# Thirty-six seven-product quads instead of thirty-two in a hybrid attention and SSD layer

## The chip, the cores and the metric

The kernel runs on one core of a Trainium2 chip. The metric is device time in microseconds, the median of several executions. Matrix products run on TensorE (PE in the profile), elementwise work on VectorE (DVE), ScalarE (ACT) and GpSimd (POOL), and SyncE (SP) issues nearly all DMAs.

## What is computed

One layer on a sequence of 256 rows of width 2048, in float32:

```python
hn = rms_norm(x, norm_w)
proj = hn @ w_in                      # 2048 x 18496
q, k, v, z_a, z_s, xbc, dt_raw, g_a, g_s = split(proj)
o_a = dilated_attention(q, k, v) * silu(z_a)
xbc = silu(causal_conv(xbc));  xs, bm, cm = split(xbc)
y = ssd_scan(xs * dt, dt * a, bm, cm) + d_skip * xs
y = rms_norm(y * silu(z_s), ssm_norm_w)
merged = sigmoid(g_a) * (o_a @ w_attn_branch) + sigmoid(g_s) * (y @ w_ssm_branch)
out = rms_norm(x + merged @ w_out, final_norm_w)
```

The change touches three of the products: y @ w_ssm_branch, with 4096 rows of weights, and v and g_a, two 2048x2048 blocks of `proj`; o_a @ w_attn_branch and merged @ w_out run in the same way.

## The kernel before, in words

**Weights.** All weights lie in one array of units of 128x1024 (512 KB), in the order in which they are used, and are streamed through five buffers (`w<n>`, tag `w`, `W_BUFS`). float32 accuracy comes from three reduced products: ACT writes a rounded copy H of a unit (`h<n>`, L264), DVE the rest L = w - H (`l<n>`, L265), and `triple` (L459 to L461) multiplies xh by H, xh by L and xl by H, where xh and xl are the same two parts of the left operand. h and l have four buffers each.

**Quads.** The five products go through `gemm_pair`. It works on a pair of 512-wide blocks of columns at once (a pass; c is 0 for the first and 2 for the second), and in steps of two 128-row tiles of weights, a quad, whose units are numbered `first + 2 * q` and one more. A pass of ssm has 16 quads, one of v, ga (the gate g_a), attn or out has 8. A plain quad is the eight products of two by two blocks, 24 matmuls of 128x512. A quad in the table `S_QUADS` is done with seven products, 21 matmuls, on sums of the blocks (a Strassen scheme). Its left sums `sx_*` are made by `turn_x`, from two tiles of the left operand, and its right sums from the units `wa` and `wb`. On DVE such a quad is: wb minus wa (L514), la (L509), lc (L509), a second sum into wb (L520), a third into wa (L522), ltt (L509) and ltu (L509); ACT makes ha, hc, htt and htu. H and L of the sums, ht and lt, have two buffers each. Four of the seven products go to accumulators of their own (`pp_*`), which `fold` (L545 to L551) adds after the pass; the others and the plain quads go to `ps_*`. After a pass the four `ps_*` are added to the folded blocks: eight half-wide (128x512) additions on DVE in all.

**Sums made early.** For ga, attn and out, `sum_jobs` makes the first two right sums of each quad during the attention phase, one half-wide subtraction each, and stores them in DRAM (`t_ga0_2`, and so on); the quad then loads `wt` from there and needs neither L514 nor L520.

**Left sums made early.** `keep_left` makes sums in a temporary, `sxt_*`, as soon as their tiles of the left operand are there, and spills them to DRAM (`sxd_*`); `fetch_left` loads them back behind a named unit: POOL copies one column of that unit's H into the new tile, which makes the DMA wait until H is done. For y and x this is done in the scan phase, for the attention result o during attention. The temporary `sxt_o6` takes a buffer of `ht`.

**Order.** A scheduler with priorities arranges each engine's instructions; the conversions of the weights (L264, L265, L508 to L522) run under `tc.high_priority(L_AHEAD)`, ahead of their place in the text. The order of quads in a pass is `A_ORDERS` for attn, `V_ORDERS` for v, `G_ORDERS` for ga, `O_ORDERS` for out (None is 0 to 7). `behind_unit(n, f)` calls f when unit n is converted, with its H as the gate.

**The opening.** The first units w0 to w4 and the blocks of x are loaded one after another by SP (L595 to L599 for w0 to w3, `load_on` for w4). Unit n is followed by the load of unit n + 4.

The stages after the opening: the projections for the scan and its groups; ssm, v; sixteen heads of attention; ga, attn, out.

Of the kernel before, what the change touches and what calls it, by code (L numbers as in the profile page):

```python
# [10 lines left out]
F32R = mybir.dt.float32r  # L11
# [4 lines left out]
P = 128  # L16
# [20 lines left out]
DT_LAG, CB_LAG, TURN_LAG, GT_LAG, Y_LAG, S_LAG, M_LAG = 2, 5, 3, 2, 11, 2, 2  # L37
Y_AFTER = 0, 0
GS_BEFORE = {0: (0, 1), 4: (2,)}
A_ORDERS = {0: (0, 1, 2, 3, 4, 6, 5, 7), 2: (0, 2, 1, 4, 3, 6, 5, 7)}  # L40
V_ORDERS = {0: None, 2: None}
G_ORDERS = {0: None, 2: None}
O_LEFT = {0: {0: (0, 3), 4: (1, 5)}, 2: {}}
O_ORDERS = {0: (0, 1, 2, 4, 3, 6, 5, 7), 2: None}
RX_UNITS = {c: 16 + c for c in range(1, 8)}
NEG = -1.0e30
S_QUADS = {
    ("ssm", 0): (5, 7, 9, 11, 13), ("ssm", 2): (5, 7, 9, 11, 13),
    ("v", 0): (2, 4, 6), ("v", 2): (2, 4, 6), ("ga", 0): (2, 4, 6), ("ga", 2): (2, 4, 6),
    ("attn", 0): (2, 4, 6), ("attn", 2): (2, 4, 6), ("out", 0): (3, 5), ("out", 2): (3, 5),  # L50
}
SX_Y = S_QUADS[("ssm", 0)]
SX_X = (2, 4, 6)
O_BEHIND = 3, 5, 7, 7
SUMS_ATT = [(t, q) for t in [(n, c) for n in ("ga", "attn", "out") for c in (0, 2)] for q in S_QUADS[t]]
ATT_QUADS = S_QUADS[("attn", 0)]
LEFT_EVERY, ATT_EVERY = 11, 4
SUM_LAG = 3

# [52 lines left out]
FIRST = {}  # L112
# [72 lines left out]
def hybrid_block(ctx: ExitStack, tc: tile.TileContext, wall, xt, x, pk_d, cst_d, fw_d, out):  # L185
# [16 lines left out]
    XT = big.tile([P, KT, 2 * S], F32R, name="XT", tag="xm")  # L202
# [11 lines left out]
    loaded = {}  # L214
# [4 lines left out]
    def behind_unit(n, f):  # L219
        on_unit.setdefault(n, []).append(f)  # L220

    def ring(name):
        return stream.tile([P, UNIT], F32, name=name, tag="w", bufs=W_BUFS)

    def spill(kept, key, name, src, shape):
        kept[key] = dram.tile([P, *shape], F32, name=name, tag=name)
        nc.sync.dma_start(kept[key], src)
# [21 lines left out]
    def load(n, cuts=(0, UNIT)):  # L249
        if n not in loaded:  # L250
            loaded[n] = stream.tile([P, UNIT], F32, name=f"w{n}", tag="w", bufs=W_BUFS)
        for a, b in zip(cuts, cuts[1:]):
            nc.sync.dma_start(loaded[n][:, a:b], wall[n, :, a:b])
# [151 lines left out]
    def keep_left(key, x, spare, t):  # L405
# [2 lines left out]
        turn_x(sx, t.rearrange("p (n m) -> p n m", n=2), x, spare)  # L408
        spill(lefts, key, f"sxd_{key[0]}{key[1]}", sx.bitcast(F32), [2, 4 - spare, P])

    def new_sx(pool, bufs, spare, name):
        return pool.tile([P, 2, 4 - spare, P], F32R, name=f"sx_{name}", tag="sx", bufs=bufs)

    def fetch_left(kept, pool, bufs, key, x, spare, u):
        def get(behind):
            sx = new_sx(pool, bufs, spare, f"{key[0]}{key[1]}")
            gp.tensor_copy(sx[:, 0, 0, 0:1], behind)
            nc.sync.dma_start(sx.bitcast(F32), lefts[key])
            kept[key[1]] = left_parts(sx, x, spare)

        behind_unit(u, get)
# [161 lines left out]
    yT = [half_kts(f"yT{n}", f"yo0{n}") for n in "ab"]  # L583
# [18 lines left out]
    def fetch(dst, src, behind):  # L602
        gp.tensor_copy(dst[:, 0:1], behind)
        nc.sync.dma_start(dst, src)

    def load_on(u):
        load(u + 4)
        if u < 3:
            nc.sync.dma_start(xr[:, 2 * u + 10 : 2 * u + 12, :], xt[:, 2 * u + 10 : 2 * u + 12, :])
        if u == 3:  # L610
            nc.sync.dma_start(pk[:, KT:], pk_d[:, KT:])
# [31 lines left out]
    with tc.tile_pool(name="ssm", bufs=2) as sp:  # L643
# [206 lines left out]
        at = big.tile([P, UNIT], F32, name="at", tag="yo1b")  # L850
# [5 lines left out]

        for n, q in enumerate(SX_X):
            behind_unit(begin + 3 + n * LEFT_EVERY, lambda behind, q=q: left_x(q, behind))

        for g in range(GROUPS):  # L860
            if g:
                for c in GS_BEFORE.get(g, ()):
                    gates(("gs", c), th_s, XT)
                group = new_group(g)
                conv(collect(project(("B", g)), f"B{g}"), 32 + g, group[0], f"B{g}")
                conv(collect(project(("C", g)), f"C{g}"), 40 + g, group[1], f"C{g}")
                after(CB_LAG, lambda a=(g, *group): make_cb(*a), 1)
            cb = group[2]
            state = {"xs": [first["xs"]], "zs": [first["zs"]]} if g == 0 else {"xs": [], "zs": []}
            for t in range(max(4 * g, 1), 4 * g + 4):  # L870
                u, i = divmod(t, 2)
                acc = project(("xs", t))
                if i == 0:
                    state["xs"].append(new_pair(u, "xs"))
                if t % 4 == 3:
                    gate = 4 * len(GS_BEFORE.get(g + 1, ()))
                    after(TURN_LAG + gate * 3 // 4, lambda a=(g, state): turn(*a))

                    y_lag = Y_LAG + gate
                    for k in range(4):  # L880
                        after(GT_LAG + k if k < 3 else y_lag - 2, lambda a=(g, k, cb, state): decays(*a))
                    after(y_lag, lambda a=(g, state): scan(*a), 1)
                    for q in (2 * g, 2 * g + 1):
                        if q in SX_Y:
                            after(
                                y_lag + 2 + Y_AFTER[1] + q % 2 * 3,
                                lambda q=q, g=g: keep_left(
                                    ("y", q), two_kts(yT, q), 1, at if g < 6 else ring(f"sxt_y{q}")
                                ),
                            )  # L890
# [25 lines left out]
    xk = ctx.enter_context(tc.tile_pool(name="xk", bufs=1))  # L916
    sx_of_x = {}

    for n, q in enumerate(SX_X[:1]):
        fetch_left(sx_of_x, xk, 1, ("x", q), two_kts(XT, q), 0, FIRST[("ssm", 2)] + 24 + 4 * n)  # L920
    with tc.tile_pool(name="xp", bufs=1) as xp:
        sxs = {}

        for q in SX_Y:
            fetch_left(sxs, xp, len(SX_Y), ("y", q), two_kts(yT, q), 1, FIRST[("ssm", 0)] + 2 * (q - 3))
# [20 lines left out]
    xl = ctx.enter_context(tc.tile_pool(name="xl", bufs=1))  # L946
# [2 lines left out]
    behind_unit(FIRST[("v", 2)] + 1, lambda behind: fetch(dc, cst_d[:, :768], behind))  # L949
    if True:  # L950
        for n, q in enumerate(SX_X[1:]):
            fetch_left(sx_of_x, xl, 2, ("x", q), two_kts(XT, q), 0, FIRST[("v", 0)] + 1 + 2 * n)
        for c in (0, 2):
            es, prods = gemm_pair(("v", c), lambda kt: XT[:, kt, :], KT, sx_of_x, c == 2, order=V_ORDERS[c])
            dst = blocks(vt, c)
            fold(prods, dst)
            for d, e in zip(dst, es):
                ve.tensor_tensor(d, e, d, ALU.add)
    sx_of_o = {}

    with tc.tile_pool(name="att", bufs=2) as ap:
        ev = ap

        oaT = [half_kts("oaTa", "yo0a")]
# [52 lines left out]
        for h in range(NH):  # L1017
            q, k = (ap.tile([P, S], F32, name=f"{n}T{h}", tag=f"{n}T", bufs=2) for n in "qk")
# [12 lines left out]

        for n, q in enumerate(ATT_QUADS):
            fetch_left(
                sx_of_o, (xk, xl, xl)[n], (1, 2, 2)[n], ("o", q), two_kts(oaT, q), 0, FIRST[("ga", 2)] + 2 * O_BEHIND[n] + 1
            )
        for c in (0, 2):
            es, prods = gemm_pair(("ga", c), lambda kt: XT[:, kt, :], KT, sx_of_x, c == 2, order=G_ORDERS[c])
            open_gate(c, es, prods)
        tick(final=True)

    with tc.tile_pool(name="fin", bufs=2) as fp:
# [42 lines left out]
        spare = big.tile([P, 8, 512], F32, name="spare", tag="yo0a")  # L1084
        sxs = {}
# [4 lines left out]
        for c0 in (0, 2):  # L1090
# [67 lines left out]
```

## Time and profile before

| | us |
|---|---|
| Time before, median of 3 runs (lowest to highest) | 1392.53 (1391.42 to 1393.67) |
| The profiled execution, its own time | 1393.24 |
| Its span, from the first to the last instruction of the profile | 1391.4 |
| TensorE busy | 1379.0 (99%) |
| VectorE busy | 1120.5 (81%) |
| ScalarE busy | 819.3 (59%) |

How to read it: a row of the timeline has the start, the length, the engine, the line and the operation, and in brackets the idle time ahead of it with the instruction or DMA that ended it. A row of the groups has the count, the busy time and the mean in ns, then the idle time ahead of the group's instructions. A row of windows has each engine's busy time in that stretch. A matmul's length in these rows is modelled and overlaps the next one's; from start to start is what counts. `w<-in_wall` is the load of a weight unit, `sxd_o<-sxt_o` a spill of left sums, `wt<-t_attn` the load of a sum made early.

### The profile page before, as it was taken

How to read it: one execution, taken by the hardware profiler on the slowest of the kernel's cores; microseconds unless marked ns; L12 is line 12 of the kernel's file. 1: busy time of each engine (PE TensorE's matmuls, PEld its weight loads, DVE VectorE, ACT ScalarE, POOL GpSimd, SP SyncE). 2: the span in 40 equal slices, each digit the busy share in tenths (PEclk: the TensorE clock that was granted, in tenths of full speed). 3: DMA queues.
4: the chain of work that ended last, by engine and by line, in shares of the span. 5: the costliest groups of instructions: out<-in, count | busy, mean ns of one | idle time of the engine just before them, and what ended most of it. 6: DMA issues, size and time to landing. Idle time of an engine off the chain costs nothing.

```text
span 1391.4 us, 20301 instructions
## 1 busy us (share of the span) xinstructions
PE 1379.0 (99%) x7290; PEld 1173.6 (84%) x7290; DVE 1120.5 (81%) x1660; ACT 819.3 (59%) x1273; POOL 86.7 (6%) x154
## 2 busy tenths in 40 slices
PE   8999999999999999999999999999999999999997
PEld 7888888888888888888888888888888888888886
DVE  6897897787787887879688896777877678779897
ACT  7656676675667676765455454545545456556454
POOL 1300000000000000000000001111110000000121
PEclk9999999999999999999999999999999999999999
DMA  9766765756575666567566667888886556766764
GB/s 342 231 187 186 238 216 171 214 185 218 178 212 177 214 187 206 187 203 252 172 227 222 231 223 242 278 268 285 293 290 194 179 180 226 245 227 215 252 240 155
DMA packets 91685, 307.75 MB, mean 221 GB/s; under 512 B 10240, under 2 KB 12224, under 8 KB 91456
## 3 DMA queue, kind: packets, MB, share of 16 engines
q1 hardware_dynamic: 90864, 305.28, 67.5%
q8 instruction: 57, 0.93, 0.3%
q10 hardware_dynamic: 720, 1.18, 0.2%
q14 instruction: 44, 0.36, 0.1%
HBM read 290.75 MB, written 15.66 MB: 220 GB/s over the span
## 4 chain that ended last, share of the span: by engine, by line
PE 95%; DVE 2%; DMA 2%; ACT 1%; issue 0%; POOL 0%; SPq 0%; POOLq 0%; DVEq 0%; ACTq 0%
PE ps_zs L317 8%; PE ps_xs L317 8%; PE ps_zs L320 4%; PE ps_za L317 4%; PE ps_k L317 4%; PE ps_q L317 4%; PE ps_xs L320 4%; PE ps_ssm L459 3%; PE ps_ssm L460 3%; PE ps_ssm L461 3%; PE ps_q L320 2%; PE ps_k L320 2%; PE ps_za L320 2%; PE ps_gs L402 2%; PE ps_gs L400 2%; PE ps_gs L401 2%
## 5 line engine op out<-in xcount | busy, mean ns | idle before, releaser
L265 DVE TENSOR_TENSOR l<-w,h 128x1024 fp32r<-128x1024 f32 (+1 forms) x420 | 506.9, 1211 | 196.1 <-ACT h L264 194.4
L264 ACT ACTIVATE h<-w 128x1024 fp32r<-128x1024 f32 (+1 forms) x420 | 438.5, 1049 | 372.6 <-issue 94.3
L317 PE MATMUL ps_zs<-XT,h 128*128 128x512 f32 x496 | 175.6, 396 | 0.0
L317 PE MATMUL ps_xs<-XT,h 128*128 128x512 f32 x496 | 175.0, 394 | 0.0
L320 PE MATMUL ps_zs<-XT,l 128*128 128x256 f32 x496 | 139.7, 282 | 0.0
L320 PE MATMUL ps_xs<-XT,l 128*128 128x256 f32 x496 | 139.4, 281 | 0.0
L317 PEld LDWEIGHTS ps_zs<-XT,h 128*128 128x128 f32 x496 | 93.0, 188 | 21.5
L317 PEld LDWEIGHTS ps_xs<-XT,h 128*128 128x128 f32 x496 | 93.0, 187 | 21.3
L320 PEld LDWEIGHTS ps_zs<-XT,l 128*128 128x128 f32 x496 | 93.6, 189 | 1.3 <-issue 1.2
L320 PEld LDWEIGHTS ps_xs<-XT,l 128*128 128x128 f32 x496 | 93.6, 189 | 0.2
L317 PE MATMUL ps_q<-XT,h 128*128 128x512 f32 x256 | 92.3, 404 | 0.0
L317 PE MATMUL ps_k<-XT,h 128*128 128x512 f32 x256 | 89.8, 395 | 0.0
L317 PE MATMUL ps_za<-XT,h 128*128 128x512 f32 x256 | 89.7, 394 | 0.0
L320 PE MATMUL ps_q<-XT,l 128*128 128x256 f32 x256 | 71.1, 278 | 0.0
L320 PE MATMUL ps_za<-XT,l 128*128 128x256 f32 x256 | 71.0, 278 | 0.0
L320 PE MATMUL ps_k<-XT,l 128*128 128x256 f32 x256 | 71.0, 277 | 0.0
L317 PEld LDWEIGHTS ps_za<-XT,h 128*128 128x128 f32 x256 | 48.0, 188 | 11.3
L317 PEld LDWEIGHTS ps_k<-XT,h 128*128 128x128 f32 x256 | 48.0, 188 | 11.2
L317 PEld LDWEIGHTS ps_q<-XT,h 128*128 128x128 f32 x256 | 48.0, 188 | 10.9
L740 ACT ACTIVATE gt<-acb,acT 128x128 f32<-128x128 f32 x128 | 43.8, 391 | 17.6 <-DMA acb<-acum_d 17.6
L320 PEld LDWEIGHTS ps_q<-XT,l 128*128 128x128 f32 x256 | 48.1, 188 | 0.4
L320 PEld LDWEIGHTS ps_k<-XT,l 128*128 128x128 f32 x256 | 48.1, 188 | 0.0
(607 smaller groups left out, 3154.0 us busy)
## 6 DMA issues: line engine op xcount, KB each, us to landing
w<-in_wall SPq DMA_DIRECT2D x416, 512.0 KB, 4.3
wa<-in_wall SPq DMA_DIRECT2D x32, 512.0 KB, 4.6
acb<-acum_d SPq DMA_DIRECT2D x32, 256.0 KB, 3.6
wb<-in_wall SPq DMA_DIRECT2D x16, 512.0 KB, 3.5
th_a<-in_wall SPq DMA_DIRECT2D x16, 512.0 KB, 5.4
th_a<-in_wall SPq DMA_DIRECT2D x16, 256.0 KB, 5.9
wb<-in_wall SPq DMA_DIRECT2D x16, 256.0 KB, 4.0
t_ga<-th_a SPq DMA_DIRECT2D x6, 512.0 KB, 4.6
```

Of the source, the lines that this page charges most:

```text
L264: ac.activation(h[:, a:b], w[:, a:b], AF.Copy)
L265: ve.tensor_tensor(l[:, a:b], w[:, a:b], h[:, a:b].bitcast(F32), ALU.subtract)
L317: pe.matmul(acc, h[:, kk, :], m, start=(kt == 0), stop=False)
L320: pe.matmul(acc[:, S:], l[:, kk, :], m[:, :S], start=False, stop=(kt == KT - 1))
L400: pe.matmul(accs[i], xh, h[:, kk], start=(kt == 0), stop=False)
L401: pe.matmul(accs[i], xh, l[:, kk], start=False, stop=False)
L402: pe.matmul(accs[i], xl, h[:, kk], start=False, stop=(kt == KT - 1))
L459: pe.matmul(acc, xh, h, start=start, stop=False)
L460: pe.matmul(acc, xh, l, start=False, stop=False)
L461: pe.matmul(acc, xl, h, start=False, stop=stop)
L740: ac.activation(g4[:, n, b], acb[:, j, b // 2 * P : b // 2 * P + P], AF.Relu, scale=-1.0, bias=sc[:, h : h + 1],)
```

## The change

`S_QUADS` gets four quads more: quad 3 in ssm's second pass, quad 5 in v's second pass and in both halves of ga. What goes with it:

- Left sums of one more pair of y's tiles (`sxd_y3`) and one more of x's (`sxd_x5`) are made in the scan phase, spilled, and fetched later. As two sizes of left sums of y are now in use, `Y_SPARE` says for each quad which it has, and the pools hold them under two tags.
- The sums made early for ga grow by two (`t_ga0_5`, `t_ga2_5`): 18 jobs, not 16.
- The new order of quads, (0, 2, 1, 4, 3, 5, 6, 7), is that of v's second pass and of both halves of ga; attn's first half gets (0, 1, 2, 4, 3, 6, 5, 7).
- The fetches of left sums stand behind other units (`O_BEHIND`, `plain_unit`).
- In the opening w4's load is placed behind unit 0: POOL copies a column of h0 into w4, and SP's DMA waits for that copy.

```diff
-A_ORDERS = {0: (0, 1, 2, 3, 4, 6, 5, 7), 2: (0, 2, 1, 4, 3, 6, 5, 7)}
-V_ORDERS = {0: None, 2: None}
-G_ORDERS = {0: None, 2: None}
+A_ORDERS = {0: (0, 1, 2, 4, 3, 6, 5, 7), 2: (0, 2, 1, 4, 3, 6, 5, 7)}
+V_ORDERS = {0: None, 2: (0, 2, 1, 4, 3, 5, 6, 7)}
+G_ORDERS = {c: (0, 2, 1, 4, 3, 5, 6, 7) for c in (0, 2)}
 S_QUADS = {
-    ("ssm", 0): (5, 7, 9, 11, 13), ("ssm", 2): (5, 7, 9, 11, 13),
-    ("v", 0): (2, 4, 6), ("v", 2): (2, 4, 6), ("ga", 0): (2, 4, 6), ("ga", 2): (2, 4, 6),
+    ("ssm", 0): (5, 7, 9, 11, 13), ("ssm", 2): (3, 5, 7, 9, 11, 13),
+    ("v", 0): (2, 4, 6), ("v", 2): (2, 4, 5, 6), ("ga", 0): (2, 4, 5, 6), ("ga", 2): (2, 4, 5, 6),
-SX_Y = S_QUADS[("ssm", 0)]
-SX_X = (2, 4, 6)
-O_BEHIND = 3, 5, 7, 7
+SX_Y = S_QUADS[("ssm", 2)]
+Y_SPARE = {q: int(q in S_QUADS[("ssm", 0)] and q in S_QUADS[("ssm", 2)]) for q in SX_Y}
+SX_X = (2, 4, 5, 6)
+O_BEHIND = 7, 14, 15, 17
...
+    def load_behind(n, behind):
+        loaded[n] = ring(f"w{n}")
+        fetch(loaded[n], wall[n], behind)
+
+    behind_unit(0, lambda behind: load_behind(4, behind))
+
     def load_on(u):
-        load(u + 4)
+        if u:
+            load(u + 4)
...
-            fetch_left(sx_of_x, xl, 2, ("x", q), two_kts(XT, q), 0, FIRST[("v", 0)] + 1 + 2 * n)
+            fetch_left(sx_of_x, xl, len(SX_X) - 1, ("x", q), two_kts(XT, q), 0, FIRST[("v", 0)] + 1 + n)
...
-                sx_of_o, (xk, xl, xl)[n], (1, 2, 2)[n], ("o", q), two_kts(oaT, q), 0, FIRST[("ga", 2)] + 2 * O_BEHIND[n] + 1
+                sx_of_o, xl if n else xk, max(1, n and len(SX_X) - 1), ("o", q), two_kts(oaT, q), 0, FIRST[("ga", 2)] + O_BEHIND[n]
```

In the instruction lists that follow, lines of the changed kernel are 1 to 11 higher than the same lines before. The counts of the whole lists: PE has 12 wide matmuls fewer, DVE 1560 instructions for 1527, ACT 1169 for 1158, SP 636 for 624.

**DVE, the later part of v's second pass.** Before, units 283 and 284 are a plain quad (q = 5) and 285 a seven-product one (q = 6):

```order
L265 TENSOR_TENSOR l283_8110<-w283_8107,h283_8109 128x1024
L265 TENSOR_TENSOR l284_8116<-w284_8113,h284_8115 128x1024
L514 TENSOR_TENSOR wb285_8144<-wb285_8144,wa285_8143 128x512
L509 TENSOR_TENSOR la285_8149<-wa285_8143,ha285_8148 128x1024
L509 TENSOR_TENSOR lc285_8153<-wb285_8144,hc285_8152 128x512
L520 TENSOR_TENSOR wb285_8144<-wb285_8144 128x512
L522 TENSOR_TENSOR wa285_8143<-wa285_8143,wb285_8144 128x1024
L509 TENSOR_TENSOR ltt285_8159<-wb285_8144,htt285_8158 128x1024
L509 TENSOR_TENSOR ltu285_8163<-wa285_8143,htu285_8162 128x1024
L265 TENSOR_TENSOR l287_8190<-w287_8187,h287_8189 128x1024
```

The same place in the changed kernel:

```order
L518 TENSOR_TENSOR wb283_8142<-wb283_8142,wa283_8141 128x512
L513 TENSOR_TENSOR la283_8147<-wa283_8141,ha283_8146 128x1024
L513 TENSOR_TENSOR lc283_8151<-wb283_8142,hc283_8150 128x512
L518 TENSOR_TENSOR wb285_8186<-wb285_8186,wa285_8185 128x512
L524 TENSOR_TENSOR wb283_8142<-wb283_8142 128x512
L526 TENSOR_TENSOR wa283_8141<-wa283_8141,wb283_8142 128x1024
L513 TENSOR_TENSOR ltt283_8157<-wb283_8142,htt283_8156 128x1024
L513 TENSOR_TENSOR la285_8191<-wa285_8185,ha285_8190 128x1024
L513 TENSOR_TENSOR ltu283_8161<-wa283_8141,htu283_8160 128x1024
L513 TENSOR_TENSOR lc285_8195<-wb285_8186,hc285_8194 128x512
L524 TENSOR_TENSOR wb285_8186<-wb285_8186 128x512
L266 TENSOR_TENSOR l287_8232<-w287_8229,h287_8231 128x1024
```

The two l's of quad 5 have become seven instructions, interleaved with the seven of quad 6.

**SP, the middle of ga's first half** (`w`, `wa`, `wb` are loads of weights, `wt` of an early sum, `sxd_o6` the spill of the last left sums of o). Before:

```order
L253 DMA w391_11416<-in_wall 128x1024
L253 DMA w392_11422<-in_wall 128x1024
L227 DMA sxd_o6_11256<-sxt_o6_11248 128x1024
L493 DMA wa393_11452<-in_wall 128x1024
L496 DMA wt393_11455<-t_ga0_4_8653 128x1024
L497 DMA wb393_11453<-in_wall 128x512
L253 DMA w395_11496<-in_wall 128x1024
L253 DMA w396_11502<-in_wall 128x1024
```

In the changed kernel:

```order
L497 DMA wa393_11476<-in_wall 128x1024
L500 DMA wt393_11479<-t_ga0_4_8695 128x1024
L501 DMA wb393_11477<-in_wall 128x512
L228 DMA sxd_o6_11316<-sxt_o6_11308 128x1024
L254 DMA w391_11520<-in_wall 128x1024
L254 DMA w392_11526<-in_wall 128x1024
L497 DMA wa395_11556<-in_wall 128x1024
L500 DMA wt395_11559<-t_ga0_5_8836 128x1024
L501 DMA wb395_11557<-in_wall 128x512
```

The three loads of quad 4 (unit 393) stand ahead of the spill now, and quad 3's (391 and 392) behind it; quad 5 (395) has three loads. On PE the first matmul that reads ltu389, of quad 2, was number 88 of the half (counting from 0) and is number 75.

**DVE, the end of attn's first half**, where `fold` begins (L548 to L551 before) and the second half's first quads (433, 434 plain, 437 with seven products) are converted. Before:

```order
L265 TENSOR_TENSOR l431_12260<-w431_12257,h431_12259 128x1024
L265 TENSOR_TENSOR l432_12266<-w432_12263,h432_12265 128x1024
L548 TENSOR_TENSOR vt_7559<-pp_attn0_2_12051,vt_7559 128x512
L549 TENSOR_TENSOR vt_7559<-pp_attn0_3_12052,vt_7559 128x512
L550 TENSOR_TENSOR vt_7559<-vt_7559 128x512
L509 TENSOR_TENSOR ltt437_12400<-wt437_12387,htt437_12399 128x1024
L551 TENSOR_TENSOR vt_7559<-vt_7559 128x512
L265 TENSOR_TENSOR l433_12347<-w433_12344,h433_12346 128x1024
L265 TENSOR_TENSOR l434_12353<-w434_12350,h434_12352 128x1024
```

In the changed kernel:

```order
L552 TENSOR_TENSOR vt_7590<-pp_attn0_2_12127,vt_7590 128x512
L266 TENSOR_TENSOR l431_12336<-w431_12333,h431_12335 128x1024
L266 TENSOR_TENSOR l432_12342<-w432_12339,h432_12341 128x1024
L553 TENSOR_TENSOR vt_7590<-pp_attn0_3_12128,vt_7590 128x512
L554 TENSOR_TENSOR vt_7590<-vt_7590 128x512
L266 TENSOR_TENSOR l433_12423<-w433_12420,h433_12422 128x1024
L555 TENSOR_TENSOR vt_7590<-vt_7590 128x512
L513 TENSOR_TENSOR ltt437_12476<-wt437_12463,htt437_12475 128x1024
L266 TENSOR_TENSOR l434_12429<-w434_12426,h434_12428 128x1024
```

The fold's first step stands ahead of l431 now, and l433 ahead of ltt437. On PE the last matmul into `pp_attn0_2`, the accumulator of that first step, stood 40 matmuls ahead of the first of attn's second half and stands 55 ahead.

In the opening, w4's load keeps its place on SP between the same two blocks of x; what is new is that it waits for POOL's copy besides the earlier DMA on its completion semaphore, the second half of w0, for which it waited before as well.

More of the change, by code (lines that the diff above doesn't have):

```diff
@@ L47 @@
 S_QUADS = {
-    ("ssm", 0): (5, 7, 9, 11, 13), ("ssm", 2): (5, 7, 9, 11, 13),
-    ("v", 0): (2, 4, 6), ("v", 2): (2, 4, 6), ("ga", 0): (2, 4, 6), ("ga", 2): (2, 4, 6),
+    ("ssm", 0): (5, 7, 9, 11, 13), ("ssm", 2): (3, 5, 7, 9, 11, 13),
+    ("v", 0): (2, 4, 6), ("v", 2): (2, 4, 5, 6), ("ga", 0): (2, 4, 5, 6), ("ga", 2): (2, 4, 5, 6),
     ("attn", 0): (2, 4, 6), ("attn", 2): (2, 4, 6), ("out", 0): (3, 5), ("out", 2): (3, 5),
 }
-SX_Y = S_QUADS[("ssm", 0)]
-SX_X = (2, 4, 6)
-O_BEHIND = 3, 5, 7, 7
+SX_Y = S_QUADS[("ssm", 2)]
+Y_SPARE = {q: int(q in S_QUADS[("ssm", 0)] and q in S_QUADS[("ssm", 2)]) for q in SX_Y}
+SX_X = (2, 4, 5, 6)
+O_BEHIND = 7, 14, 15, 17
 SUMS_ATT = [(t, q) for t in [(n, c) for n in ("ga", "attn", "out") for c in (0, 2)] for q in S_QUADS[t]]
-ATT_QUADS = S_QUADS[("attn", 0)]
+ATT_QUADS = sorted({*S_QUADS[("attn", 0)], *S_QUADS[("attn", 2)]})
 LEFT_EVERY, ATT_EVERY = 11, 4
@@ L409, in keep_left, with plain_unit @@
         spill(lefts, key, f"sxd_{key[0]}{key[1]}", sx.bitcast(F32), [2, 4 - spare, P])
+    def plain_unit(tag, q):
+        return FIRST[tag] + 2 * max(n for n in range(q + 1) if n not in S_QUADS[tag])
     def new_sx(pool, bufs, spare, name):
-        return pool.tile([P, 2, 4 - spare, P], F32R, name=f"sx_{name}", tag="sx", bufs=bufs)
+        return pool.tile([P, 2, 4 - spare, P], F32R, name=f"sx_{name}", tag=f"sx{spare}", bufs=bufs)
     def fetch_left(kept, pool, bufs, key, x, spare, u):
@@ L887, in hybrid_block @@
                                 lambda q=q, g=g: keep_left(
-                                    ("y", q), two_kts(yT, q), 1, at if g < 6 else ring(f"sxt_y{q}")
+                                    ("y", q), two_kts(yT, q), Y_SPARE[q], at if g < 6 else ring(f"sxt_y{q}")
                                 ),
@@ L924, in hybrid_block @@
         for q in SX_Y:
-            fetch_left(sxs, xp, len(SX_Y), ("y", q), two_kts(yT, q), 1, FIRST[("ssm", 0)] + 2 * (q - 3))
+            fetch_left(sxs, xp, sum(s == Y_SPARE[q] for s in Y_SPARE.values()), ("y", q), two_kts(yT, q), Y_SPARE[q], plain_unit(("ssm", 0), q - 3 if q in S_QUADS[("ssm", 0)] else 12))
         for c in (0, 2):
```

## The prediction, made before the changed kernel ran

> **What bounds the kernel now.** The head of the page comes first: busy time by engine, then the shares of the chain that ended last, then one row of its list of DMA issues.
>
> ```profile
> PE 1379.0 (99%) x7290; PEld 1173.6 (84%) x7290; DVE 1120.5 (81%) x1660; ACT 819.3 (59%) x1273; POOL 86.7 (6%) x154
> ...
> PE 95%; DVE 2%; DMA 2%; ACT 1%; issue 0%; POOL 0%; SPq 0%; POOLq 0%; DVEq 0%; ACTq 0%
> ...
> w<-in_wall SPq DMA_DIRECT2D x416, 512.0 KB, 4.3
> ```
>
> TensorE is busy for 99% of the span and is 95% of the chain. So a matmul less is time less, as long as nothing makes TensorE wait. The view of waits, for PE alone, says how often it does now.
>
> ```profile
> PE ps_first L365 <- ACT h L264: 2.5, 2, 1.7
> PE warm L588 <- DVE ssq L585: 1.4, 1, 1.4
> PE ps_attn L460 <- DVE l L265: 0.3, 1, 0.3
> ```
>
> These rows are the sum, the count and the longest. 3.9 us stand in the opening and 0.3 at one place near the end. Between them TensorE never waits, so the gain is bounded by matmuls removed plus 0.3, and the danger is that the makers of its operands fall behind.
>
> **The matmuls.** A seven-product quad is 21 matmuls of 128x512 instead of 24. Four quads change, so 12 go; the changed program's list on PE has 12 wide ones fewer. The price of one is the distance from the first matmul of v's first pass to the first of its second, in the timeline of PE:
>
> ```profile
> 751.91 0.39 PE L459 MATMUL ps_v<-h,XT 128*128 128x512 f32 x1
> 793.39 0.39 PE L459 MATMUL ps_v<-h,XT 128*128 128x512 f32 x1
> ```
>
> A pass with three seven-product quads is 5 x 24 + 3 x 21 = 183 matmuls: 41.48 us / 183 = 0.2267 us. Twelve are **2.72 us**. (The 0.39 us in the rows is a pipelined matmul's own length, not its price.) The Trainium skill, "TensorE: Matmul & The Clock Gate", section "Wait — 56ns, not 53.3ns?", has 215.7 ns from start to start for this width on a warm array; by that, 12 would be 2.59 us. The row of this kernel is 5% above it, and the sum goes by the row.
>
> **The price on DVE: v's second pass.** For what it saves, a seven-product quad gives DVE more to do. Without a sum made earlier it has seven instructions (L514 to L522 and four of L509), from 776.60 to 783.36 here; a plain quad has two (L265).
>
> ```profile
> 776.60 0.69 DVE L514 TENSOR_TENSOR wb<-wb,wa 128x512 f32<-128x512 f32 x1 [1.04 <-DMA wb<-in_wall]
> ...
> 783.36 2.40 DVE L265 TENSOR_TENSOR l<-w,h 128x1024 fp32r<-128x1024 f32 x2
> ...
> 791.25 0.68 DVE L551 TENSOR_TENSOR vt<-vt 128x512 f32<-128x512 f32 x1
> 791.85 0.68 DVE L958 TENSOR_TENSOR vt<-ps_v,vt 128x512 f32<-128x512 f32 x1
> ...
> 795.36 2.35 DVE L265 TENSOR_TENSOR l<-w,h 128x1024 fp32r<-128x1024 f32 x2
> 797.63 1.22 DVE L509 TENSOR_TENSOR la<-wa,ha 128x1024 fp32r<-128x1024 f32 x1
> ```
>
> So: 6.76 us the seven-product quad, 797.63 - 795.36 = 2.27 the plain one, and 0.60 from one half-wide start to the next, eight of which fold a pass (4.8). A pass of v costs DVE 3 x 6.76 + 5 x 2.27 + 4.8 = 36.4 us now, under TensorE's 41.5. The second pass will cost 4 x 6.76 + 4 x 2.27 + 4.8 = **40.9**, and TensorE's 180 matmuls are 180 x 0.2267 = **40.8**. Nothing is to spare on average; whether TensorE waits is settled by how far DVE is ahead. That lead I work out by adding the spacings in the changed program's order (1.14 us wide, 0.60 half-wide), with DVE through the fold at 795.36 as now and TensorE's first matmul at 793.39. l275 is the fifth after the fold: 795.36 + 3 x 1.14 + 2 x 0.60 = 800.0; its first matmul is number 40 of the pass, at 793.39 + 40 x 0.2267 = 802.5: lead 2.5. ltt283, 12 wide and 7 half-wide steps on, comes at 817.9 and is wanted as number 127, at 822.2: 4.3. ltu285, the last, 8 and 2 further on, comes at 828.2 and is wanted as number 179, at 834.0: 5.8. What DVE itself waits for comes off these leads; over both passes that is
>
> ```profile
> L265 DVE TENSOR_TENSOR l<-w,h 128x1024 fp32r<-128x1024 f32 x20 | 24.1, 1220 | 2.1 <-ACT h L264 2.1
> ...
> L509 DVE TENSOR_TENSOR lc<-wb,hc 128x512 fp32r<-128x512 f32 x6 | 4.1, 687 | 1.6 <-ACT hc L508 1.6
> L514 DVE TENSOR_TENSOR wb<-wb,wa 128x512 f32<-128x512 f32 x5 | 3.5, 692 | 2.8 <-DMA wb<-in_wall 2.8
> ```
>
> 6.5 us, 3.3 a pass, 1.1 to each of six seven-product quads, or 4 x 1.1 = 4.4 in a pass with four. One more such wait before l275 leaves 1.4. The new quad's own load can follow ltt281 only (five weight buffers), about 809.1; with the page's 4.3 us it lands at 813.4, where DVE comes by at 812.6: 0.8 lost out of 4.3. I take **0** for v; the ends are 0 (PE waits for nothing in v now, so there is no stall to win back) and 4.5 lost (rival C).
>
> **The gate halves.** Their sums are made during attention, so a quad is five DVE instructions:
>
> ```profile
> 1152.36 1.22 DVE L509 TENSOR_TENSOR la<-wa,ha 128x1024 fp32r<-128x1024 f32 x1
> 1153.50 0.68 DVE L509 TENSOR_TENSOR lc<-wb,hc 128x512 fp32r<-128x512 f32 x1
> 1154.10 1.22 DVE L522 TENSOR_TENSOR wa<-wa,wt 128x1024 f32<-128x1024 f32 x1
> ...
> 1141.46 1.23 DVE L509 TENSOR_TENSOR ltu<-wa,htu 128x1024 fp32r<-128x1024 f32 x1 [0.66 <-ACT htu L508]
> ```
>
> la, wa, ltt, ltu at 1.14 and lc at 0.60 are 5.15; a half costs 4 x 5.15 + 4 x 2.27 + 4.8 = 34.5 against 40.8, so the average is safe. One place is tight. The last row is ltu389, done at 1142.69. Its H half waits for ACT, and ACT for a left sum's spill, whose temporary holds the buffer:
>
> ```profile
> 1135.79 0.33 SPq L227 DMA_DIRECT2D sxd_o<-sxt_o  x1
> 1140.37 1.06 ACT L508 ACTIVATE htu<-wa 128x1024 fp32r<-128x1024 f32 x1 [0.82 <-DMA sxd_o<-sxt_o]
> 1126.14 0.58 PE L459 MATMUL ps_ga<-h,XT 128*128 128x512 f32 x1
> 1146.47 0.39 PE L460 MATMUL ps_ga<-ltu,XT 128*128 128x512 f32 x1
> ```
>
> TensorE wants ltu389 at 1146.47, as number 88 of its half. In the changed order it is number 75: 13 x 0.2267 = 2.9 us sooner, 1143.5. The lead of 3.8 becomes **0.8**. In the new order on SP three loads of quad 4 stand ahead of that spill, which could hold it back; I take no loss, since SP had issued it 4.6 us before its use and the three loads had been issued by then. If the landing took 5.5 us (the sum's load in the next fence) about 0.1 is lost, with 6.7 (the weight unit in the opening's fence) 1.3. Elsewhere in both halves the same adding leaves 1.8 or more.
>
> **The wait in attn.** The 0.3 us stands at l435, early in attn's second half. DVE reached l435 late, having waited 1.96 us at ltt437 for ACT, and ACT for the load of a premade sum:
>
> ```profile
> 1261.79 0.50 PE L460 MATMUL ps_attn<-l,oaTa 128*128 128x512 f32 x1 [0.26 <-DVE l L265]
> ```
> ```profile
> 1248.16 1.23 DVE L509 TENSOR_TENSOR ltt<-wt,htt 128x1024 fp32r<-128x1024 f32 x1 [1.96 <-ACT htt L508]
> ```
> ```profile
> 1247.07 1.06 ACT L508 ACTIVATE htt<-wt 128x1024 fp32r<-128x1024 f32 x1 [3.01 <-DMA wt<-t_attn]
> ```
> ```profile
> 1241.42 5.54 DMA wt<-t_attn
> ```
>
> Between ltt437 and l435 DVE has nothing but work: l's, the first half's additions and its merge. In the changed order the last matmul into the accumulators that the fold begins with stands 55 matmuls ahead of attn's second half, not 40, so the fold may begin 15 x 0.2267 = 3.4 us sooner, and l433 is made ahead of ltt437. Even if ltt437 waits as long again, DVE is more than a microsecond sooner at the merge, and the 0.26 goes: **0.26** gained. Late next there is l436, right behind l435 on DVE and sooner by the same. Bounds: 0.26 gained, or 1 lost if the sum's load, now asked for by other neighbours, is later still.
>
> **What costs nothing.** ssm's second pass: DVE is busy 67 us of the 84 in the row below; the new quad adds 6.76 - 2.27, and 71.5 still lie beside TensorE. The two more left sums in the scan phase cost DVE one half-wide, four 128-wide subtractions and a split each, about 2.4 us by the rows below (0.69 + 4 x 0.28 + 0.55); idles at l, of 2.2 us in the third row, take part of them, and PE's list of waits has no l that came late there. Four extra half-wide sums in attention (2.4 us) go among idles of the same kind. If that cover failed, each would cost its own length at most.
>
> ```profile
> 668.00:752.00 84.00, 84.00 (x372) 69.54 (x372) 67.04 (x70) 42.45 (x45) 0.29 (x1) 1.00 0.63 208
> ```
> ```profile
> L433 DVE TENSOR_TENSOR sxt_y<-yT 128x512 f32<-128x512 f32 x1 | 0.7, 685 | 0.0
> L274 DVE TENSOR_TENSOR yT<-at,yT 128x128 fp32r<-128x128 f32 x2 | 0.6, 284 | 0.0
> L274 DVE TENSOR_TENSOR sxt_y<-sxt_y 128x384 fp32r<-128x384 f32 x1 | 0.6, 552 | 0.0
> ```
> ```profile
> 249.06 1.23 DVE L265 TENSOR_TENSOR l<-w,h 128x1024 fp32r<-128x1024 f32 x1 [2.21 <-ACT h L264]
> ```
>
> The opening: w4 will wait for h0's first half, done at 4.45 in the row below. But its issue, the row at 6.65, already waits for w0's second half, as the semaphore list of the order shows. TensorE's 1.73 us there come from w1, whose transfer (the last row, from the chain in order of time) had begun ahead of it. I take **0**; the ends are under D, and as much lost if the gate on POOL is slow.
>
> ```profile
> 3.82 0.63 ACT L264 ACTIVATE h<-w 128x512 fp32r<-128x512 f32 x1
> ...
> 6.65 0.44 SPq L253 DMA_DIRECT2D w<-in_wall  x1
> ...
> 10.47 1.19 PE L365 MATMUL ps_first<-yTa,h 128*128 128x512 f32 x4 [1.73 <-ACT h L264]
> ```
> ```profile
> 3.05 6.71 DMA w<-in_wall
> ```
>
> **The sum.** The profiled execution took 1393.24 us, its span 1391.4 with 1.84 around it: 1393.24 - 2.72 - 0.26 = 1390.26. The median of the three runs shown is 0.71 lower, 1392.53, and so the forecast: 1392.53 - 2.98 = **1389.6**.
>
> **Rivals.**
> - **A**, the forecast: all twelve matmuls gained, no new wait. Own range 1388.9 to 1390.3 (the attn wait kept or gone, and the spread of the three runs on either side). Chance 0.58.
> - **B**, small waits: ltu389 or l275 late by 0.8 to 2.2 us, as the leads above allow. 1390.4 to 1391.8, say 1391.0. Chance 0.23. For it: a lead of 0.8 in a place that hangs on one DMA. Against it: DVE is done early at all other places.
> - **C**, the other side: DVE becomes the bound. Its idle time grows with the seven-product quads and the leads don't absorb it: v's second pass 40.9 + 4.4 - 40.8 = 4.5 late, and each gate half by the idles below, (9.3 + 2.9) / 6 = 2.0 a quad, 34.5 + 4 x 2.0 - 40.8 = 1.7. Together 7.9 - 2.98 = +4.9, about 1397.5; it ends above the old time once 3.0 are lost. For it speaks the sum of 40.9 against 40.8; against it, that the waits for ACT in the rows are DVE running ahead, which end by themselves when it is behind. Chance 0.10. The Trainium skill, "Perfetto Trace Analysis", section "Identifying the Most-Contended Engine", calls matmul busy time a poor measure, and judges TensorE by the share of LDWEIGHTS and DVE by occupancy: 84% to 81% on this page, two engines almost level, which speaks for C; the missing waits of PE speak against it.
>
> ```profile
> L265 DVE TENSOR_TENSOR l<-w,h 128x1024 fp32r<-128x1024 f32 x19 | 23.1, 1222 | 9.3 <-ACT h L264 9.3
> ...
> L509 DVE TENSOR_TENSOR ltu<-wa,htu 128x1024 fp32r<-128x1024 f32 x6 | 7.3, 1224 | 2.9 <-ACT htu L508 2.7
> ```
>
> - **D**, the opening does gain: w4 really starts later than I say, and w1, freed from it, lands sooner. At most half of the 1.73, so 1388.7. Chance 0.09. Against it: the load is issued at 6.65 already, most of the way through w1's.
>
> **How the numbers follow.** About 0.2% (2.8 us) is what a measurement of this kernel can tell from no change; faster begins under 1389.7. A is split by that line, a little more than half of it below; with D that gives faster 0.43. The rest of A, B and a small part of C are within 0.2%: 0.48. Slower by more is the rest of C: 0.09. The range, 1388.5 to 1392.2, takes in A, B and most of D.
>
> **What would show it.** In the profile after: PE's instructions 12 fewer and its busy time less by some 2.7; v's second pass from first matmul to first matmul of q near 40.8; no PE wait in v, at ltu389 or at ps_attn; w4's issue still near 6.65. I am wrong if the waits of PE list ps_v or pp_ga behind DVE with more than 1 us, or if DVE's lead in ga is gone because the spill of sxd_o6 is issued after 1136.

## The result, and the profile after

The changed kernel takes **1390.49 us** (median of 22 runs, 1389.69 to 1392.87); the kernel before, measured beside it, 1392.49 (22 runs, 1391.29 to 1394.78). The ratio is 0.9986 with a 95% interval of 0.9979 to 0.9992: 2.0 us faster, 0.14%. The forecast was 1389.6, 2.9 us faster. So two thirds of the forecast gain arrived; the time lies in the range, within 0.2% of before.

The head of the page of the changed kernel, then its view of waits for PE (sum, count, longest):

```profile
span 1389.4 us, 20366 instructions
...
PE 1377.6 (99%) x7278; PEld 1172.2 (84%) x7278; DVE 1139.7 (82%) x1692; ACT 825.5 (59%) x1283; POOL 96.6 (7%) x164
```
```profile
PE ps_first L366 <- ACT h L265: 1.9, 2, 1.3
PE warm L592 <- DVE ssq L589: 1.4, 1, 1.4
```

PE lost 12 instructions, as forecast, but only 1.4 us of its busy time, not 2.7. There is no wait in v, in ga or in attn. What kept half of the saving is therefore hidden in PE's busy time, where the view of waits has nothing to show. The place is found by cutting the span at the first matmul of each stage. These rows of the timeline are of before and of the changed kernel, the first matmul of dt (the end of the opening) and of ssm (the end of the scan):

```profile
30.19 1.11 PE L342 MATMUL ps_dt<-yTa,h 128*128 128x512 f32 x4
583.54 0.50 PE L459 MATMUL ps_ssm<-h,yTa 128*128 128x512 f32 x1
```
```profile
29.95 1.33 PE L343 MATMUL ps_dt<-yTa,h 128*128 128x512 f32 x5
585.07 0.50 PE L463 MATMUL ps_ssm<-h,yTa 128*128 128x512 f32 x1
```

From dt to ssm it is 553.35 before and 555.12 after: the scan phase, in which no quad is changed, became **1.77 us longer**. The table has all stages, worked out in this way from the profiles of four kernels (two of them from the experiments below); v is counted to the first matmul of k0, and attention from there.

| stage, us | before | changed | whole13 | v0_too |
|---|---|---|---|---|
| opening | 30.19 | 29.95 | 29.75 | 28.56 |
| scan | 553.35 | 555.12 | 553.70 | 553.64 |
| ssm | 168.36 | 167.68 | 167.68 | 167.68 |
| v | 88.60 | 87.94 | 87.94 | 94.42 |
| attention | 285.63 | 285.17 | 285.17 | 285.63 |
| ga | 84.93 | 83.58 | 83.58 | 83.58 |
| attn, first half | 41.48 | 41.48 | 41.48 | 41.48 |
| attn, second half | 44.25 | 43.66 | 44.20 | 43.92 |

ssm gains 0.68, v 0.66, ga 1.35: together 2.69 for 12 matmuls. Attention gains 0.46, attn 0.59, the opening 0.24. That is 3.98; less the 1.77 of the scan it is 2.21, and the rest of the program gives 0.2 back, so that the span is 2.0 shorter.

What the scan phase lost shows in PE's timeline. Before, the 16 products of the scan of group 2 (`yp`, float32, each two records) stand together:

```profile
285.35 0.39 PE L317 MATMUL ps_xs<-XT,h 128*128 128x512 f32 x1
285.58 0.28 PE L320 MATMUL ps_xs<-XT,l 128*128 128x256 f32 x1
285.70 0.39 PE L317 MATMUL ps_zs<-XT,h 128*128 128x512 f32 x1
286.02 2.82 PE L777 MATMUL yp<-gt,xdt 128*64 128x256 f32 x32
```

In the changed kernel one of them stands 26 us earlier, alone among the weight matmuls:

```profile
260.03 0.40 PE L318 MATMUL ps_xs<-XT,h 128*128 128x512 f32 x1
260.26 0.39 PE L318 MATMUL ps_zs<-XT,h 128*128 128x512 f32 x1
260.58 0.65 PE L788 MATMUL yp<-gt,xdt 128*64 128x256 f32 x2
261.16 0.39 PE L321 MATMUL ps_xs<-XT,l 128*128 128x256 f32 x1
261.38 0.40 PE L318 MATMUL ps_xs<-XT,h 128*128 128x512 f32 x1
```

Without it, a wide matmul on h and a half-wide one on l take 0.35 (285.35 to 285.70 above). With it they take 261.38 - 260.26 = 1.12. The lone one costs 0.77. Group 3 has another (at 318.04). That makes 1.54 of the 1.77; the other 0.2 stand in the 11 us ahead of the lone one of group 2, where weight matmuls start a little further apart (the last section). That no engine waits is why the view of waits is empty: PE executes the same matmuls, in an order that costs more.

### The profile page after: what moved, and what is told of

The parts are those of the page before. It is cut to its first block, busy times and chain, and to the rows that moved or that the text cites. A ratio compares the mean times of both kernels' runs of the same rounds, so it can differ in the third digit from the quotient of the medians.

```text
span 1389.4 us, 20366 instructions
## 1 busy us (share of the span) xinstructions
PE 1377.6 (99%) x7278; PEld 1172.2 (84%) x7278; DVE 1139.7 (82%) x1692; ACT 825.5 (59%) x1283; POOL 96.6 (7%) x164
## 4 chain that ended last, share of the span: by engine, by line
PE 98%; DMA 0%; DVE 0%; POOL 0%; SPq 0%; ACT 0%; issue 0%; POOLq 0%; DVEq 0%; ACTq 0%
PE ps_zs L318 8%; PE ps_xs L318 8%; PE ps_zs L321 4%; PE ps_q L318 4%; PE ps_za L318 4%; PE ps_k L318 4%; PE ps_xs L321 4%; PE ps_ssm L463 3%; PE ps_ssm L464 3%; PE ps_ssm L465 3%; PE ps_q L321 2%; PE ps_k L321 2%; PE ps_za L321 2%; PE ps_gs L403 2%; PE ps_gs L402 2%; PE ps_gs L401 2%
## 5 line engine op out<-in xcount | busy, mean ns | idle before, releaser
L266 DVE TENSOR_TENSOR l<-w,h 128x1024 fp32r<-128x1024 f32 (+1 forms) x412 | 497.2, 1211 | 177.1 <-ACT h L265 174.9
L265 ACT ACTIVATE h<-w 128x1024 fp32r<-128x1024 f32 (+1 forms) x412 | 430.0, 1048 | 353.4 <-issue 91.3
L512 ACT ACTIVATE ha<-wa 128x1024 fp32r<-128x1024 f32 x36 | 38.0, 1057 | 21.1 <-PE ps_v L465 7.2
```

What stands on the lines that cost most here:

```text
L265: ac.activation(h[:, a:b], w[:, a:b], AF.Copy)
L266: ve.tensor_tensor(l[:, a:b], w[:, a:b], h[:, a:b].bitcast(F32), ALU.subtract)
L512: ac.activation(h, src, AF.Copy)
```

## The experiments

Theory 1: the two yp matmuls that the order put ahead, alone, cost what is missing. Theory 2: it is the DVE and DMA work of the two added left sums in the scan phase. For the rest of the prediction the questions are whether DVE's sum of 40.9 against 40.8 is a real limit, and whether the opening took part. "whole13" is the changed kernel with another spacing of the x sums, on which most of the others are built. Ratios are to the kernel before, run beside each.

**whole13, whole14.** The left sums of x are made every 13, or 14, units; all 36 quads and all left sums remain, and the 16 yp of every group stand together.

```diff
-LEFT_EVERY, ATT_EVERY = 11, 4
+LEFT_EVERY, ATT_EVERY = 13, 4
```

> The changed kernel with its x sums spread over 13 units instead of 11, so that the 16 yp matmuls of every group stand together on PE again; the left sums of x5 and y3 are still made in the scan phase and all 12 matmuls are still saved. Theory 1 (the changed kernel lost its missing part to two yp matmuls that stand alone among weight matmuls, about 0.85 us each): scan phase as long as before, 1.7 us under the changed kernel, about 1388.8. Theory 2 (the loss is DVE and DMA work of the two added left sums): still about 1390.5, and the scan phase still 1.7 longer than before.

Measured: 1389.05 (ratio 0.9975, 0.9965 to 0.9985), scan 553.70. Theory 1 holds, and theory 2 falls: the added sums are still made, and 1.42 of the 1.77 us are gone.

> The changed kernel with its x sums every 14 units: another spread at which the 16 yp matmuls of every group stand together. If it is the lone matmuls that the changed kernel loses by, and not something that 13 units have of their own: scan phase 553.3 to 553.8, as with 13 units, and 1388.5 to 1389.5. If 13 was a lucky spread: scan phase near 555.1 as in the changed kernel, 1390.5.

Measured: 1389.58 (0.9981, 0.9971 to 0.9990), scan 554.06. The time is under the changed kernel's again, but the scan misses the expectation by 0.3: 0.7 over before remains, with no lone yp matmul. So lone yp matmuls are most of the loss. The traces show where the rest is: whole13 loses its 0.35 between about 189 and 210 us, whole14 the same there and once more between about 249 and 271, in stretches where the weight matmuls start further apart (the last section).

**head1, head2.** The price by itself: on whole13, in seven groups, the first one (or two) of the yp matmuls are issued a step earlier.

```diff
-                    after(y_lag, lambda a=(g, state): scan(*a), 1)
+                    after(y_lag - 1, lambda a=(g, state, True): scan(*a), 1)
+                    after(y_lag, lambda a=(g, state, False): scan(*a), 1)
```

> The kernel with 13 units, and in seven of the eight scan groups the first yp matmul issued one step earlier, alone, the other 15 as before. Theory 1: 7 x 0.85 = 6 us more than with all 16 together, about 1394.8, the block of 15 no shorter than that of 16. Theory 2 (left sums): no more than 0.1 us each, about 1389 to 1391.

Measured: 1394.24 (1.0013, 1.0004 to 1.0022); scan 559.09, 5.39 over whole13, or **0.77 for each** of seven. PE's timeline for group 4, the lone one and the block behind it:

```profile
424.97 0.65 PE L789 MATMUL yp<-gt,xdt 128*64 128x256 f32 x2
...
431.30 2.81 PE L789 MATMUL yp<-gt,xdt 128*64 128x256 f32 x30
```

The block of 15 is as long as the block of 16 was (2.81 and 2.82).

> The same with the first two yp matmuls early. In groups 0, 1 and 3 they stand side by side, in groups 2, 4, 5 and 6 each alone. If it is the broken pair that costs (two matmuls that use half of the columns each run side by side), a pair costs 0.3 to 0.5 us a group and its block of 14 is shorter by 0.34; two alone cost 1.3 to 1.4. If it is the change from one kind of matmul to the other that costs, whatever the number, a pair costs the 0.85 of a single one.

Measured, in one execution: 1395.02, scan 558.39, 4.69 over whole13. The rows are of group 0, where two stand side by side:

```profile
159.49 0.65 PE L789 MATMUL yp<-gt,xdt 128*64 128x256 f32 x4
...
165.82 2.39 PE L789 MATMUL yp<-gt,xdt 128*64 128x128 f32 x28
```

Two take 0.65 like one, and 14 take 2.39, 0.43 less than 16. Each writes half of the 128 output columns (128*64 in the rows), and two such run side by side. A lone one thus costs a full place of its own and saves none in the block, besides the change from one kind of matmul to the other and back; for a pair 0.77 - 0.43 = 0.34 is left. Both parts of the explanation are needed: the change of kind costs even the pair something. Two that stand alone in one group cost 2 x 0.77 - 0.43 = 1.11 by this, under the 1.3 to 1.4 that was expected. Added up, three pairs and four such groups make 5.5, and the scan lost 4.69; in the trace each of these places has its price, and the 0.8 comes back elsewhere in the phase, by weight matmuls that start closer together.

**before_lone.** The kernel before with `LEFT_EVERY` 10, which happens to set one yp matmul of group 1 apart.

> The kernel before with the left sums of x made every 10 units instead of 11; no quad is changed. In group 1 one yp matmul then stands alone. If a lone one costs what it did in the run with seven of them: scan phase 0.8 longer than before (553.35 us), everything behind it unchanged. If it costs only together with the added left sums: unchanged.

Measured, in one execution: 1395.85, scan 554.98, 1.63 longer. No quad and no left sum is added, and still there is a loss, so it is not the change's content that costs but the order. Around the lone matmul it is 0.78; the other 0.85 comes behind it without another lone one, in two stretches (to about 224, and from about 248 to 268 us) in which the wide weight matmuls start further apart, as in the last section. In this execution attn's second half was also 1.4 longer, with waits for la and l there. The single time is no measure of the one matmul.

**v0_too.** On whole13, v's first pass gets its quad 5 as well.

```diff
-    ("v", 0): (2, 4, 6), ("v", 2): (2, 4, 5, 6), ("ga", 0): (2, 4, 5, 6), ("ga", 2): (2, 4, 5, 6),
+    ("v", 0): (2, 4, 5, 6), ("v", 2): (2, 4, 5, 6), ("ga", 0): (2, 4, 5, 6), ("ga", 2): (2, 4, 5, 6),
```

> The kernel above with quad 5 of v's first pass also done with seven products, in the order of the second pass (37 quads). DVE's sum is then 40.9 us against PE's 40.8 in two passes one after the other. If its lead carries it (smallest lead in the changed kernel's second pass 1.9 us): 0.68 less than the kernel above, about 1388.1, no PE wait in v. If the lead is used up (the other-side rival of the prediction, 1.1 us of DVE idle for each seven-product quad): up to 4.4 more by the end of the second pass, about 1392, with ps_v waiting for DVE.

Measured: 1395.39 (1.0015, 1.0006 to 1.0023), 6.3 slower than whole13. v takes 94.42 where it should take 87.94 - 0.68: 7.2 us lost, 3.3 in the first pass and 3.9 in the second, more than the 4.4 that was expected at most. The prediction's rival C is what happens here. DVE's groups from v's start to 834, then its windows' two halves (busy times of PE, PEld, DVE, ACT and POOL):

```profile
L518 DVE TENSOR_TENSOR wb<-wb,wa 128x512 f32<-128x512 f32 x7 | 4.8, 688 | 7.5 <-DMA wb<-in_wall 7.5
```
```profile
749.90:792.00 42.10, 40.23 (x173) 31.70 (x172) 38.16 (x43) 22.58 (x26) 4.33 (x4) 1.00 0.61 215
792.00:834.00 42.00, 39.66 (x170) 31.24 (x169) 37.64 (x43) 21.59 (x25) 0.00 (x0) 1.00 0.57 191
```

DVE is busy for 75.8 of these 84.1 us. For 7.5 it stands still at the head of its queue, before the first subtraction, for a wb that has not landed. PE sees it as waits:

```profile
PE ps_v L463 <- ACT hc L512: 1.8, 2, 1.1
...
PE ps_v L464 <- DVE l L266: 1.1, 1, 1.1
PE pp_v L464 <- DVE la L513: 0.5, 1, 0.5
```

These three are 3.4 of the 7.2. Part of the rest is in steps too small for the view: from v's start to k0 PE is busy for 90.22 us, and 87.26 would do.

Why then does the changed kernel lose nothing in v's second pass, with the same sum of 40.9? What differs is the lead with which DVE enters. DVE's first la of the pass and PE's first matmul on it, in the changed kernel's second pass and in v0_too's first:

```profile
795.04 1.22 DVE L513 TENSOR_TENSOR la<-wa,ha 128x1024 fp32r<-128x1024 f32 x1
```
```profile
800.36 0.39 PE L464 MATMUL pp_v<-la,XT 128*128 128x512 f32 x1
```
```profile
753.42 1.22 DVE L513 TENSOR_TENSOR la<-wa,ha 128x1024 fp32r<-128x1024 f32 x1
```
```profile
756.01 0.39 PE L464 MATMUL pp_v<-la,XT 128*128 128x512 f32 x1
```

From its end to its use the lead is 4.1 us in the one and 1.4 in the other, where DVE has ssm's merge ahead of it. That the lead decides is argued from these rows; no run changes it alone.

**v0_only, v0_late, v0_pool.** Three variants to see what of v0_too it is.

> Four seven-product quads in v's first pass and three in the second (36 quads, 13 units for the x sums). Rate: the first pass loses its 3 us as with 37 quads and the second, with 36.4 us of DVE work, none: v near 91, about 1392. If one tight pass can be borne wherever it stands: v near 87.9, 1389.

Measured, in one execution: 1393.24, v 91.54, 3.6 over whole13. The pass right behind ssm loses 3.6 by itself; the second one, with three such quads, loses nothing more and wins nothing back.

> The kernel with 37 quads, in v's first pass two plain quads first (order 0, 1, 2, 4, 3, 5, 6, 7). In the kernel with the first seven-product quad second, SP stood 8.1 us at a left sum's gate with quad 2's second unit queued behind it. If that start is the cause (SP's queue): the wait falls behind plain quads' loads already issued, DVE keeps its lead, and most of the 7 us comes back, about 1388.5 to 1390. If it is the sum on DVE (40.9 against 40.8 twice, with a wait for wb in each quad): still 1393 or more.

Measured: 1396.58 (1.0027, 1.0015 to 1.0038), v 94.86. The order of the first quads, and with it SP's 8.1 us at a left sum's gate, is not the cause. It moves the loss: the first pass loses 1.7 now (42.46 from first matmul to first matmul, where 40.80 would do) and the second 5.9.

v0_pool leaves the quads and moves one DVE instruction to GpSimd:

```diff
-                    ve.tensor_tensor(wt[:, :512], wt[:, :512], wa[:, :512], ALU.subtract)
+                    (gp if tag[0] == "v" else ve).tensor_tensor(wt[:, :512], wt[:, :512], wa[:, :512], ALU.subtract)
```

> The kernel with 37 quads and the subtraction into the lower half of wb, in v's two passes, on GpSimd instead of DVE: DVE's sum falls by 4 x 0.6 = 2.4 to 38.5 us a pass, under PE's 40.8. If DVE's rate is what lost 6.5 us in v: most of it comes back, v from its start to the first k near 88 to 90 us (94.4 with DVE alone, 87.9 with 36 quads), 1388.5 to 1390.5. If it is the landing of wb, which the subtraction waits for on either engine: DVE waits for POOL in place of the DMA, and v stays at 93 or more, 1394 or more.

Measured: 1391.08 (0.9982, 0.9973 to 0.9992), v 88.63: 5.8 of the 7.2 us come back. POOL's group from v's start to 838, and PE's only wait in v:

```profile
L518 POOL TENSOR_TENSOR wb<-wb,wa 128x512 f32<-128x512 f32 x8 | 14.9, 1864 | 59.0 <-DMA wb<-in_wall 56.4 <-DVE wa L526 2.6
```
```profile
PE pp_v L463 <- ACT htu L512: 0.8, 1, 0.8
```

One subtraction takes POOL 1864 ns, to DVE's 688, and POOL now does the waiting for wb. v is as long as was expected if DVE's rate were the limit (the time is 0.6 over what was), but DVE did not get less busy:

```profile
750.00:792.00 42.00, 42.00 (x187) 34.75 (x187) 40.77 (x41) 23.50 (x27) 10.42 (x8) 1.00 0.65 215
792.00:834.00 42.00, 41.16 (x184) 33.59 (x183) 40.63 (x39) 23.03 (x26) 5.99 (x4) 1.00 0.67 219
```

It is busy for 81.4 us of these 84.0, more than in v0_too: some of its other instructions became longer (lc from 684 to 1202 ns in the mean, la from 1217 to 1355), which takes up the time of the subtractions that left. What the edit took from DVE is the 7.5 us at the head of its queue: it no longer waits for wb at all. So the loss was that wait, and not the amount of work: in v0_too the instructions behind it then ran with no wait of their own. With 37 quads this is no better than whole13's 36.

**old_w4, w4_only.** whole13 with w4's load as before, and the kernel before with nothing but w4's load changed (the lines of `load_behind` and `load_on` in the diff above).

> The kernel with 13 units, with w4's load where it was before (no copy on POOL). If the opening gains nothing from the change (the forecast): about 1389.0 like the kernel with 13 units, SP's issue of w4 near 6.7 in both, and the start of dt inside the spread of the profiles so far (28.5 to 30.0 with the new load, 30.2 in the one with the old). If it gains (rival D): dt starts at 30 or later, and the time is 0.5 to 0.9 longer.

Measured: 1389.53 (0.9975, 0.9965 to 0.9985): the ratio is whole13's to four digits. dt starts at 29.16.

> The kernel before with nothing changed but w4's load behind unit 0. Forecast: no difference, 0.0 +- 0.3 us. Rival D: 0.5 to 0.9 faster, dt starting near 29.3 instead of 30.2.

Measured: 1392.27 (0.9994, 0.9985 to 1.0003): no difference that can be told, but an interval that reaches from 2.1 us faster to 0.4 slower, and so does not exclude rival D's 0.5 to 0.9. SP's row for w4, in this kernel:

```profile
6.92 0.53 SPq L604 DMA_DIRECT2D w<-in_wall  x1
```

It is issued 0.3 later than at 6.65 before, if anything. dt starts at 29.95 here, and anywhere from 28.4 to 30.0 in the profiles of kernels with the new load; with the old load it starts at 29.16 to 30.19 in three. The opening varies from one execution to the next by more than the 0.24 in the table.

**old_attn.** whole13 with attn's first half in the old order of quads.

> The kernel with 13 units, with attn's first half in its old order of quads. If the order is what moved the fold, the wait at l435 is 0.26 us or more, and attn's second half is 0.3 to 0.6 longer; if the wait has to do with where the sum's load lands, no difference beyond 0.1.

Measured, in one execution: 1389.28, attn's second half 44.67 with a wait of 0.26 for l. In whole13 it is 44.20, and in the ten profiles with the new order 43.66 to 44.20; in the four with the old one 44.14 to 45.70 (before has 44.25, w4_only 44.14, before_lone 45.70). So the new order is worth some 0.4, with a spread of the same size. The wait for l stands in all four profiles with the old order, and in three of the ten with the new (whole13 0.26, v0_pool 0.24, v0_too 0.16).

## Why the prediction was right or wrong, point by point

- **Twelve matmuls at 0.2267, 2.72 us: right.** The three stages with more seven-product quads gave 2.69.
- **v's second pass, no wait: right, and for the reason given.** This is DVE's l275 in the changed kernel; its end by the prediction's adding was 800.0:

```profile
798.76 1.22 DVE L266 TENSOR_TENSOR l<-w,h 128x1024 fp32r<-128x1024 f32 x1
```

  It ends at 799.98 and is used at 803.30: 3.3 in place of 2.5, since PE begins the pass 0.85 later by the loss in the scan. The smallest lead of the pass is 1.9, at l287. That nothing is to spare was right too: v0_too and v0_only lost 3.6 us a pass where DVE came in with little lead, close to the 4.5 of rival C. As C has it, it was idle time of DVE that the lead didn't absorb (7.5 us at wb in v0_too's two passes); the amount of work, which the sum of 40.9 stands for, was not it, as v0_pool shows. C was wrong about the place: not the passes that the change touched.
- **The gate halves, no wait: right, with the tight place misjudged.** SP issued the spill of sxd_o6 at about the time that was expected (1135.79 before), but it landed sooner:

```profile
1135.27 0.33 SPq L228 DMA_DIRECT2D sxd_o<-sxt_o  x1
1138.39 1.06 ACT L512 ACTIVATE htu<-wa 128x1024 fp32r<-128x1024 f32 x1 [0.97 <-DMA sxd_o<-sxt_o]
```

  3.1 us from issue to use, not 4.6, and ltu389 ended 2.3 ahead of PE instead of 0.8. The smallest lead was in the second half, 0.45 at l415, where the prediction said 1.8 or more.
- **The wait in attn, 0.26 gained: right in kind, for the reason given.** ltt437 waits as long as before, but behind more of the fold:

```profile
1247.70 1.22 DVE L513 TENSOR_TENSOR ltt<-wt,htt 128x1024 fp32r<-128x1024 f32 x1 [1.75 <-ACT htt L512]
```

  The half gained 0.59 in this profile; over the profiles about 0.4, and the wait itself came back in three of ten.
- **The opening, 0: not contradicted.** w4's issue did not move by more than 0.3 us, and the two runs of w4 alone show no difference; their intervals are too wide to exclude a gain like D's.
- **The scan phase, 0: wrong, and this is the step that failed.** "What costs nothing" priced the two added left sums by DVE's idle time and by the leads ahead of PE, and there they do cost nothing. It did not ask in what order PE would now do its own work. That order came out otherwise, and two yp matmuls went ahead alone: 2 x 0.77 = 1.54 of the 1.77 us. (That it was the added sums that moved the scheduler's choice is likely, since another spacing of them moves it back; no run takes them out.) Without them (whole13) the kernel is at 1389.05, 0.5 under the forecast.
- **Attention: 0.46 gained that nothing in the prediction had.** It is a matter of PE's order too; see the last section.

The rivals: the time is that of B (1390.4 to 1391.8), but not by B's mechanism, which was small waits; the view lists none there. That the loss of 1.77 did not move the time further from the forecast is luck: attention's 0.46, and what attn and the opening gave beyond the forecast in this profile, set off part of it.

## What to carry to other kernels

When a change adds work on one engine under a scheduler, compare the order on every engine, above all the one that is the bound, over the whole program and not only around the edit: a matmul that changes places costs time without any wait to point to it. Where an engine's sum is level with the bound's, look for the lead with which it enters the stretch: the same sum was free behind a light pass and cost 3.6 us behind a heavy one. And look at what stands at the head of its queue: the cost was a wait for a load, and it went when another engine did the waiting. Cut the span at the first matmul of each stage, in both profiles: differences of 0.05 us repeat there, while total times spread by over 1 us.

## What the runs showed of the hardware that was not expected

Matmuls of the projections do not always start at the same distance, with no wait and the same clock. The rows are the first and the last wide matmul of the projection q1, 15 pairs of a wide and a half-wide one apart, in before and in the changed kernel:

```profile
851.82 0.40 PE L317 MATMUL ps_q<-XT,h 128*128 128x512 f32 x1
...
857.12 0.40 PE L317 MATMUL ps_q<-XT,h 128*128 128x512 f32 x1
```
```profile
851.86 0.39 PE L318 MATMUL ps_q<-XT,h 128*128 128x512 f32 x1
...
857.05 0.40 PE L318 MATMUL ps_q<-XT,h 128*128 128x512 f32 x1
```

5.30 us in the one, 5.19 in the other: 2% slower, over some 30 us around this place, which makes the 0.46 us that attention gained. In both kernels the granted clock from 840 to 870 is 1.00 and PE is busy for all of it. It is slow in the profiles of before, w4_only, before_lone, v0_too, v0_late, v0_only and v0_pool (attention 285.63 or 285.64) and not in those of the changed kernel, whole13, whole14, old_w4, old_attn, head1 and head2 (285.17): it repeats from execution to execution, and it goes with PE's order. In all seven of the fast ones, and in none of the slow ones, one wide matmul of the next projection (`ps_za`) stands ahead of its turn; these rows are of the changed kernel:

```profile
843.51 0.40 PE L318 MATMUL ps_k<-XT,h 128*128 128x512 f32 x1
843.75 0.40 PE L318 MATMUL ps_za<-XT,h 128*128 128x512 f32 x1
843.99 0.28 PE L321 MATMUL ps_k<-XT,l 128*128 128x256 f32 x1
```

Such a stretch is also what is left of the scan's loss in whole13 and whole14. The rows are two wide matmuls of `zs`, 31 pairs apart, in before and in whole13:

```profile
191.93 0.40 PE L317 MATMUL ps_zs<-XT,h 128*128 128x512 f32 x1
...
202.68 0.39 PE L317 MATMUL ps_zs<-XT,h 128*128 128x512 f32 x1
```
```profile
191.54 0.40 PE L318 MATMUL ps_zs<-XT,h 128*128 128x512 f32 x1
...
202.47 0.40 PE L318 MATMUL ps_zs<-XT,h 128*128 128x512 f32 x1
```

10.75 us and 10.93. Here it is the slower kernel, whole13, in which a wide matmul (of `zs`, at 188.60) stands ahead of its turn where the stretch begins. So a matmul out of turn goes with a change of pace, either way. No run moves such a matmul alone, so this is no more than what the traces have in common, and the cause stays open.
